# Attention keys in chunks of 128, 128 and 16 instead of 96, 96 and 80, with the small queries of two heads worked on together

## The chip, the cores and the metric

The kernel runs on one core of a Trainium2 chip. The metric is the device time of one execution in microseconds (us). The engines are called as in the profile: PE (matmul; PEld is its weight load), DVE (vector), ACT (scalar activations), POOL (GpSimd) and SP (which only issues DMAs here).

## What is computed

One layer of an encoder over 272 tokens: 16 meta tokens and 256 real ones, 2048 features. All numbers are fp32. Eight heads of group A attend to a window of the token grid and to the meta tokens; eight heads of group B are latent attention over all tokens. Meta tokens are dropped at the end.

```python
hn = rmsnorm(h, mix_norm_g)
q_a, k_a, v_a, cq, ckv, k_pe = split(hn @ w_in)
out_a = neighbourhood_attention(rmsnorm(q_a), rmsnorm(k_a), v_a, na_rpb, na_meta_bias)
out_b = mla_attention(cq, ckv, k_pe, ...)        # softmax(q k^T) v, q and k of 192 dims
mix = concatenate([rmsnorm(out_a), rmsnorm(out_b)])
h = h + mix @ w_out
h = h + conv_glu(rmsnorm(h), w_gate, w_up, conv_w, conv_b, w_down)
return h[:, N_META:]
```

The convolution of the MLP reaches one position to each side, so of the meta tokens only the last one's output is needed. The kernel keeps the real tokens first and the meta tokens behind them in reverse, and computes queries for 258 positions (`NT`): 256 real ones and two more, the *small queries*. Keys and values exist for all 272 (`L`).

## The kernel before

**Numbers.** Every fp32 matrix is split into a rounded fp32r part `hi` and the rest `lo`, and a product is three matmuls (hi hi, hi lo, lo hi; `product3`, `mm3`). Weights come by DMA in pieces of 128 x 1024 into five `raw` buffers; ACT copies each half piece of 512 columns to `whi`, DVE subtracts and writes `wlo`, each with three buffers. PE then streams the 128 x 128 blocks (lines 369 to 371, in the MLP lines 1268 and 1269).

**Order.** The program is recorded by a planner (`Flow`): each piece of work is a generator that asks for an engine with a cost (`ACT`, `TT`, `TS`, `STT`, `COPY`, `RED`, `PTT`, `MM`, `TR` hold the costs), waits for events, and takes buffers from `Slots`. The planner starts whatever can start first by these costs. So the order on each engine is fixed when the program is built, and a change of costs or buffers moves the instructions around it. On the chip each engine takes its queue in this order and waits by semaphores.

**Stages.** First the latent projections, then four pairs of heads, then the output projection (`out_b`, `out_a`) and the MLP. A pair streams the weights of group A's queries, of group B's queries, keys and values (`up`), and of group A's keys and values; its attention work stands between these matmuls on PE. In the order of PE's queue the pairs read as weights with attention blocks among them. `na_head` and `mla_head` spawn three jobs a head: two query tiles of 128 rows (`na_tile`, `mla_tile`) and the small queries of two rows (`na_small`; `mla_tile` with `rows` = 2). Each job makes scores with PE, a softmax with DVE and ACT in `p`, and transposes the probabilities:

```python
CW = 96
LP = 3 * CW
def p_transposed(p, rows, PT, q0, slots):
    yield from TR([(pt[:CW, j * P : j * P + rows], p[:rows, j * CW : (j + 1) * CW]) for j in range(3)])
    ...
    yield from split_plain(PT[:, 0, :, q0 : q0 + rows], PT[:, 1, :, q0 : q0 + rows], src)
```

So the 272 keys are three chunks of 96 rows, the last padded with zeros. `PT` holds the transposed probabilities of one head for all 258 queries, hi and lo, three chunks. `attend` multiplies them with the values: three chunks of three matmuls are nine matmuls of 258 columns, the result is split to `oa` or `ob`, and POOL adds its square to `sum_a` or `sum_b` for the group's RMS norm. `ones_sum` of `sum_b` (a matmul with ones) starts the chain that scales the output projection of group B; the planner lets head h attend after head h - 1 has been added.

The norms of the queries need sums of squares over the 128 or 192 dims. For the tiles ACT sums them along transposed rows; for the small queries PE multiplies `sq2` and `sqm` with a column of ones in fp32, two matmuls a pair in group A (`na_queries`), four in group B (`mla_queries`).

## Time and profile before

| | |
|---|---|
| three runs, median (lowest to highest) | 1144.75 us (1144.36 to 1145.29) |
| the profiled execution's own time | 1144.01 us |
| its span, first to last instruction | 1142.2 us |
| busy: PE, PEld, DVE, ACT, POOL | 1136.7, 1071.1, 812.8, 659.8, 107.7 us |
| matmul records on PE | 8160 |
| chain that ended last | PE 97% |
| clock granted to PE | 1.0 in full |

The latent projections take the first 30 us, the four pairs the time from 30 to about 310 us, 62 us each; then come the output projection and, to the end, the MLP. A matmul's duration in the profile overlaps with the next one's, so what a matmul costs is read from the distance between starts. In a timeline row a group of instructions in sequence has one start, one length and its count.

### The profile page before, as it was taken

What the parts mean: (1) busy time and instruction counts of PE and PEld (TensorE: products, weight loads), DVE (VectorE), ACT (ScalarE), POOL (GpSimd) and SP (SyncE); (2) the same over time, 40 slices, a digit from 0 to 9 for tenths busy, and PEclk for the clock granted to TensorE, in tenths of its full rate; (3) what the DMA queues carried; (4) which work ended last, traced back from release to release, by engine and by line L of the source; (5) the groups of instructions that cost most, each with busy time, mean ns of one, the idle gap of its engine ahead of it and who ended that gap; (6) DMA issues with size and microseconds to landing.
All of it is one profiled execution on the core that took longest, in us unless ns stands there. A gap on an engine that the chain in (4) does not pass through costs nothing.

```text
span 1142.2 us, 21907 instructions
## 1 busy us (share of the span) xinstructions
PE 1136.7 (100%) x8160; PEld 1071.1 (94%) x8160; DVE 812.8 (71%) x1724; ACT 659.8 (58%) x1430; POOL 107.7 (9%) x118
## 2 busy tenths in 40 slices
PE   9999999999999999999999999999999999999998
PEld 8999999999999999999999999999999888888888
DVE  8779696979977866777677767776776755555553
ACT  8677787868645655555555555555555544444442
POOL 0010001010224600010001000100010000000000
PEclk9999999999999999999999999999999999999999
DMA  9543434444555556555555555555555566766662
GB/s 330 184 133 111 158 130 140 139 143 132 188 180 177 181 176 195 189 180 188 186 189 178 192 187 188 177 192 187 187 180 190 174 193 205 211 198 195 198 195 74
DMA packets 63054, 203.62 MB, mean 178 GB/s; under 512 B 6882, under 2 KB 13412, under 8 KB 62948
## 3 DMA queue, kind: packets, MB, share of 16 engines
q1 hardware_dynamic: 62804, 202.11, 55.1%
q8 instruction: 64, 1.05, 0.4%
q14 instruction: 42, 0.34, 0.1%
q10 hardware_dynamic: 144, 0.12, 0.0%
HBM read 200.10 MB, written 2.10 MB: 177 GB/s over the span
## 4 chain that ended last, share of the span: by engine, by line
PE 97%; ACT 1%; issue 1%; DVE 1%; DMA 0%; POOL 0%; DVEq 0%; POOLq 0%
PE bank L1268 27%; PE bank L369 16%; PE bank L370 16%; PE bank L371 16%; PE bank L1269 14%; PE bank L246 5%; PE bank L252 2%; ACT whi L206 1%; ACT hl L206 0%; DMA vecs<-in_vecs 0%; DVE hl L218 0%; DVE wlo L210 0%; ACT scr L206 0%; POOL kr L234 0%; ACT bias L206 0%
## 5 line engine op out<-in xcount | busy, mean ns | idle before, releaser
L210 DVE TENSOR_TENSOR wlo<-raw,whi 128x512 fp32r<-128x512 f32 (+1 forms) x737 | 521.7, 718 | 260.1 <-ACT whi L206 257.2
L206 ACT ACTIVATE whi<-raw 128x512 fp32r<-128x512 f32 (+1 forms) x737 | 458.2, 629 | 396.3 <-PE bank L1268 179.3
L369 PE MATMUL bank<-hl,whi 128*128 128x258 f32 (+1 forms) x1232 | 357.4, 290 | 0.5 <-ACT whi L206 0.3
L370 PE MATMUL bank<-hl,whi 128*128 128x258 f32 (+1 forms) x1232 | 351.4, 285 | 0.1
L371 PE MATMUL bank<-hl,wlo 128*128 128x258 f32 (+1 forms) x1232 | 350.2, 284 | 0.5 <-DVE wlo L210 0.4
L1268 PE MATMUL bank<-hl,whi 128*128 128x512 f32 x704 | 246.3, 392 | 0.0
L371 PEld LDWEIGHTS bank<-hl,wlo 128*128 128x128 f32 x1232 | 235.2, 191 | 1.7 <-DVE wlo L210 1.1
L369 PEld LDWEIGHTS bank<-hl,whi 128*128 128x128 f32 x1232 | 232.7, 189 | 2.7 <-ACT whi L206 1.0
L370 PEld LDWEIGHTS bank<-hl,whi 128*128 128x128 f32 x1232 | 234.3, 190 | 0.5 <-DVE hl L218 0.3
L1268 PE MATMUL bank<-act,whi 128*128 128x512 f32 x660 | 228.8, 391 | 0.0
L1269 PE MATMUL bank<-hl,wlo 128*128 128x256 f32 x704 | 197.8, 281 | 0.0
L1269 PE MATMUL bank<-act,wlo 128*128 128x256 f32 x660 | 185.1, 280 | 0.0
L1268 PEld LDWEIGHTS bank<-hl,whi 128*128 128x128 f32 x704 | 132.1, 188 | 28.7
L1268 PEld LDWEIGHTS bank<-act,whi 128*128 128x128 f32 x660 | 123.5, 187 | 26.8
L1269 PEld LDWEIGHTS bank<-hl,wlo 128*128 128x128 f32 x704 | 132.9, 189 | 0.0
L1269 PEld LDWEIGHTS bank<-act,wlo 128*128 128x128 f32 x660 | 125.0, 189 | 0.0
L234 POOL TENSOR_TENSOR mt<-mt,s 128x256 f32<-128x256 f32 x44 | 41.6, 966 | 459.6 <-ACT mt L206 459.6
L218 DVE SCALAR_TENSOR_TENSOR mt<-mt,vecs,mt 128x256 f32<-128x256 f32 x88 | 40.3, 479 | 0.0
L369 PE MATMUL bank<-ob,whi 128*128 128x258 f32 x128 | 37.1, 290 | 0.0
L370 PE MATMUL bank<-ob,whi 128*128 128x258 f32 x128 | 36.4, 284 | 0.0
L371 PE MATMUL bank<-ob,wlo 128*128 128x258 f32 x128 | 36.0, 281 | 0.0
L206 ACT ACTIVATE scr<-scr 128x272 f32<-128x272 f32 x77 | 32.6, 423 | 5.1 <-DVE scr L218 3.7
(207 smaller groups left out, 1196.3 us busy)
## 6 DMA issues: line engine op xcount, KB each, us to landing
raw<-in_w_gate SPq DMA_DIRECT2D x88, 512.0 KB, 4.3
raw<-in_w_up SPq DMA_DIRECT2D x88, 512.0 KB, 4.4
raw<-in_w_down SPq DMA_DIRECT2D x80, 512.0 KB, 4.4
raw<-in_w_in SPq DMA_DIRECT2D x54, 512.0 KB, 4.2
raw<-in_w_out SPq DMA_DIRECT2D x32, 512.0 KB, 4.3
raw<-in_w_down SPq DMA_DIRECT2D x16, 256.0 KB, 3.3
raw<-in_w_cq SPq DMA_DIRECT2D x7, 512.0 KB, 5.6
bias<-in_na_bias SPq DMA_DIRECT2D x8, 272.0 KB, 4.3
```

The source lines that it names most:

```text
L206: nc.scalar.activation(out, in_, f, **kw)
L210: nc.vector.tensor_tensor(out, a, b, op)
L218: nc.vector.scalar_tensor_tensor(out, a, s, b, op0, op1)
L234: nc.gpsimd.tensor_tensor(out, a, b, op)
L246: nc.tensor.matmul(o, l, r, start=start, stop=stop)
L252: nc.tensor.transpose(o, i, ident[:n, :n])
L369: nc.tensor.matmul(ps, whi, xhi, start=start, stop=False)
L370: nc.tensor.matmul(ps, whi, xlo, start=False, stop=False)
L371: nc.tensor.matmul(ps, wlo, xhi, start=False, stop=stop)
L1268: nc.tensor.matmul(ps, whi, x, start=start, stop=False)
L1269: nc.tensor.matmul(ps[:, :n], wlo, x[:, 0, :], start=False, stop=stop)
```

## The change

The keys are cut into chunks of 128, 128 and the 16 meta tokens. The third chunk is used as one matmul with three copies of the meta tokens in its rows: 32 rows apart stand hi, hi and lo of the values against hi, lo and hi of the probabilities (rows between are zero; `KP` = 80 rows), so one matmul gives all three products. `attend` then has one matmul for the meta tokens and six for the two chunks, seven instead of nine; in group A the six cover only the 256 real queries, since the small queries there attend to meta tokens alone.

The copies are made where the probabilities are normalised (`normalized` writes the 256 columns and then three times the 16) and where group A's values are scaled (`na_values`). `split_chunks` splits the transposed chunks in two steps each on ACT and DVE instead of one.

The small queries of two heads are worked on once a pair, as four rows (head 0's two, head 1's two). Their queries stand in `qs`, where each head's two columns have zeros at the other head's place, so that the scores of both heads accumulate in the same four rows. POOL copies them there (`small_queries`). The sums of squares are two or four fp32r matmuls of two columns, of a split that POOL makes (`small_sums`). `mla_small` and `na_small` run after the second head's keys are there, and both heads' `attend` wait for them (`ev_few`). `PT` holds two heads; there are two instead of three one-head tiles.

```diff
-CW = 96
-LP = 3 * CW
+CW = 32
+KP = 2 * CW + N_META
+LP = L + 3 * CW
...
+    def thrice(row):
+        out = row[:, L : L + 3 * CW].rearrange("p (i x) -> p i x", i=3)[:, :, :N_META]
+        return out, repeated(row[:, SEQ:L], 3)
...
-    pts = Slots(tiles(apool, 3, [CW, 2, 3, NT], "pt", F32R))
+    pts = Slots(tiles(apool, 2, [P, 2, 5, NT], "pt", F32R))
+    qss = tiles(apool, 2, [P, 36], "qs", F32R)
+    sq8 = tiles(apool, 2, [P, 8], "sq8")
+    sq8r = tiles(apool, 2, [P, 2, 8], "sq8r", F32R)
...
+    def chunks_transposed(t, pt):
+        yield from TR(
+            [(pt[:, :P], t[:, :P]), (pt[:, P : 2 * P], t[:, P:SEQ]), last_transposed(t, pt)]
+        )
+    def last_transposed(t, pt):
+        return pt[:KP, 2 * P : 3 * P], t[:, L : L + KP]
+    def split_chunks(out, src, lo):
+        yield from ACT(out[:, 0:2], src[:, 0:2], AF.Copy)
+        yield from TT(out[:, 3:5], src[:, 0:2], out[:, 0:2].bitcast(F32), ALU.subtract)
+        yield from split_last(out[:, 2], src[:, 2], lo)
+    def split_last(out, src, lo):
+        yield from ACT(out[:KP], src[:KP], AF.Copy)
+        e = slice(lo * CW, lo * CW + N_META)
+        yield from TT(out[e], src[e], out[e].bitcast(F32), ALU.subtract)
+    def normalized(p, w, a, n=P):
+        out, src = thrice(p)
+        if a < SEQ:
+            yield from TS(p[:n, a:SEQ], p[:n, a:SEQ], w, None, ALU.mult)
+        yield from TS(out[:n], src[:n], w, None, ALU.mult)
...
-        items = []
-        for j in range(3):
+        items = [(o_, V[:KP, 2], PT[:KP, 2], True, False)]
+        for j in range(2):
             items += product3(
-                o_, (Vh[:, j, :], Vl[:, j, :]), (PT[:, 0, j, :], PT[:, 1, j, :]), j == 0, j == 2
+                o[:, :n], (V[:, j], V[:, 3 + j]), (PT[:, j, :n], PT[:, 3 + j, :n]), False, j == 1
             )
...
+    def small_queries(s):
+        for ev in s.ev_qs:
+            yield ev
+        t = s.qs[:, :24].rearrange("p (l c x) -> p l c x", l=2, c=2)
+        for i in range(2):
+            yield "pool", 150
+            nc.gpsimd.tensor_copy(t[:, i, :, 0:2], s.q[:, :, i, SEQ:NT])
+        fl.set(s.ev_small)
+    def small_sums(q8, n):
+        f, r = q8
+        yield "pool", 150
+        nc.gpsimd.tensor_copy(r[:, 0, : 4 * n], f[:, : 4 * n])
+        yield from PTT(
+            r[:, 1, : 4 * n], f[:, : 4 * n], r[:, 0, : 4 * n].bitcast(F32), ALU.subtract
+        )
...
+            [(ss[:4, 0:2], r[:, i, 4 * g : 4 * g + 4], ones_r[:, 0:2], (g, i) == m[0], (g, i) == m[-1])
+             for g, i in m]
...
-        yield from TS(p[:, :L], p[:, :L], w[:, 2:3], None, ALU.mult)
+        yield from normalized(p, w[:, 2:3], 0)
...
-        yield from p_transposed(p, 2, PT, SEQ, few)
+        pt = yield from one(tps)
+        yield from TR([last_transposed(p, pt)])
+        fl.put(probs, p)
+        yield from split_small(PT, 2, pt)
...
+        if c == 1:
+            fl.spawn(na_small(s, pr, s.PT, s.ev_few))
         for ev in done:
             yield ev
         fl.put(bias, B)
+        yield s.ev_few
...
-            yield from MM([(ss[:2, c : c + 1], sq2[:, c, :], ones[:, 0:1], True, True) for c in range(2)])
+        ss = yield from small_sums(q8, 1)
...
+        for c in range(2):
+            k, kp = s.k[c], s.kp[c]
+            q = [s.qs[:, 12 * i + 4 * c : 12 * i + 4 * c + 4] for i in range(3)]
+            items += product3(S_, q[:2], (k[:, 0, :], k[:, 1, :]), c == 0, False)
+            items += [(S_, q[2], kp[:, 0, :], False, False), (S_, q[2], kp[:, 1, :], False, c == 1)]
```

In the built program PE has 8055 matmul instructions instead of 8119, DVE 1779 instructions instead of 1726, ACT 1397 instead of 1353, and POOL 163 instead of 123; the DMAs are the same but for the shape of `meta_bias`. Line numbers of the changed kernel are 4 to 12 higher at the helpers (`TT` 214 for 210, `MM` 250 for 246, `TR` 256 for 252, `mm3` 381 to 383 for 369 to 371).

More of the change, by code (lines that the diff above doesn't have):

```diff
@@ L868, in na_head @@
         yield ev_B
[L869 to L870 removed]
+        if c == 0:
+            s.PT = yield from one(pts)
+            fl.set(s.ev_PT)
+        yield s.ev_PT
+        done = [Event() for _ in range(2)]
         for i in range(2):
[L872 to L873 removed]
+            fl.spawn(na_tile(s, c, i, B, s.PT, done[i]))
+        if c == 1:
+            fl.spawn(na_small(s, pr, s.PT, s.ev_few))
         for ev in done:
@@ L954, in mla_queries @@
             fl.put(tps, pt)
-        ss = yield from one(sps)
-        for c in range(2):
-            yield from MM(
-                [(ss[:2, c : c + 1], sq2[:, c, :], ones[:, 0:1], True, False),
-                 (ss[:2, c : c + 1], m[:, c, :], ones[:, 0:1], False, True)]
-            )
-        fl.put(sqm, m)
+        ss = yield from small_sums(q8, 2)
         v = yield from one(v6)
```

254 lines of the change are left out of this document (157 added, 97 removed).

## The prediction

> **What bounds the kernel now.** I read the page first, then the waits of PE, then the stretches of one pair of heads, then PE's rows one by one. The page and PE's waits:
>
> ```profile
> PE 1136.7 (100%) x8160; PEld 1071.1 (94%) x8160; DVE 812.8 (71%) x1724; ACT 659.8 (58%) x1430; POOL 107.7 (9%) x118
> PE 97%; ACT 1%; issue 1%; DVE 1%; DMA 0%; POOL 0%; DVEq 0%; POOLq 0%
> PE bank L371 <- DVE wlo L210: 0.4, 2, 0.2
> ```
>
> PE is the bound: it is 97% of the chain that ended last, and it waits for almost nothing. An instruction taken off PE's queue is worth the distance to the next start that it took, if the other engines keep up. Whether they do is read from the stretches of the third pair (columns: stretch and its length, then busy time of PE, PEld, DVE, ACT, POOL):
>
> ```profile
> 188.00:197.40 9.40, 9.40 (x80) 9.12 (x80) 4.67 (x12) 8.15 (x33) 0.76 (x1) 1.00 0.37 119
> 197.40:240.00 42.60, 42.60 (x353) 41.37 (x353) 41.48 (x120) 35.21 (x102) 3.88 (x3) 1.00 0.35 113
> 240.00:252.00 12.00, 12.00 (x102) 11.84 (x101) 7.53 (x15) 7.35 (x18) 1.49 (x2) 1.00 0.60 199
> ```
>
> From 197.4 to 240 DVE has 1.1 us free in 42.6; in the other 21.4 us it has 9.2 free. So in the attention part DVE is nearly as full as PE, and only the split weights that it has ready save PE from waiting. Where that reserve runs out in this pair, and where it is still there:
>
> ```profile
> 204.01 0.69 DVE L210 TENSOR_TENSOR wlo<-raw,whi 128x512 fp32r<-128x512 f32 x1
> 204.55 0.29 PE L370 MATMUL bank<-hl,whi 128*128 128x272 f32 x1
> 204.75 0.40 PE L371 MATMUL bank<-hl,wlo 128*128 128x272 f32 x1
> 236.00 0.68 DVE L210 TENSOR_TENSOR wlo<-raw,whi 128x512 fp32r<-128x512 f32 x1
> 239.31 0.28 PE L371 MATMUL bank<-hl,wlo 128*128 128x258 f32 x1
> ```
>
> The half piece split at 204.01, called C below, is done at 204.70 and used at 204.75: L371 starts 0.20 us behind L370 where 0.125 is usual. The one split at 236.00 lies 2.63 us before its use.
>
> **PE's part of the change.** Its prices are distances between starts:
>
> ```profile
> 223.03 1.24 PE L246 MATMUL bank<-pt,mv 96*128 96x258 f32 x9
> 224.11 0.29 PE L369 MATMUL bank<-hl,whi 128*128 128x272 f32 x1
> ```
>
> Next the two small trios behind each other (`2*96`: transposes of two rows; `128*2 128x16`: small scores of group A), and a trio of transposes from 128 rows:
>
> ```profile
> 228.87 0.29 PE L371 MATMUL bank<-hl,wlo 128*128 128x272 f32 x1
> 229.09 0.30 PE L252 MATMUL bank<-consts,p 2*96 2x2 f32 x3
> 229.32 0.23 PE L246 MATMUL bank<-nak,naq 128*2 128x16 f32 x3
> 229.40 0.37 PE L369 MATMUL bank<-hl,whi 128*128 128x272 f32 x1
> 229.61 0.29 PE L370 MATMUL bank<-hl,whi 128*128 128x272 f32 x1
> ```
>
> ```profile
> 212.38 0.29 PE L371 MATMUL bank<-hl,wlo 128*128 128x272 f32 x1
> 212.51 0.49 PE L252 MATMUL bank<-consts,p 128*96 128x128 f32 x3
> 212.76 0.37 PE L369 MATMUL bank<-hl,whi 128*128 128x272 f32 x1
> 212.97 0.29 PE L370 MATMUL bank<-hl,whi 128*128 128x272 f32 x1
> ```
>
> Attends: nine matmuls take 224.11 - 223.03 = 1.08 us, 0.12 each; seven take 0.84. Four heads a pair (two of each group): 4 x 0.24 = 0.96 us.
>
> Transposes: the two small trios cost 229.61 - 228.87 less two ordinary distances of 0.125, so 0.49, of which 0.08 are the scores' (229.32 to 229.40) and 0.41 the transposes'; three from 128 rows cost 212.97 - 212.38 - 0.25 = 0.34. In a pair, group A's two small trios (0.82) become one transpose. No lone one is in the trace; a third of a trio is 0.11, its bounds are 0.03 and the whole trio's 0.34. I take 0.11, since each further one in a trio only adds its own time: gain 0.71 (0.48 to 0.79). Group B's two trios (0.82) become one trio from 128 rows: gain 0.48. The transposes of the 128-row tiles and of the values keep their number.
>
> The small sums of squares of group B:
>
> ```profile
> 202.44 0.29 PE L371 MATMUL bank<-hl,wlo 128*128 128x272 f32 x1
> 202.66 0.19 PE L246 MATMUL bank<-consts,cols 128*2 128x1 f32 x2
> ...
> 203.16 0.29 PE L370 MATMUL bank<-hl,whi 128*128 128x272 f32 x1
> ```
>
> These four fp32 matmuls cost 203.16 - 202.44 - 0.25 = 0.47; four fp32r ones replace them. The nearest row is the small scores' trio 128x16: 0.08 to the next start, and 0.085 lost at the one after (229.40 to 229.61). Four then cost about 0.2, and 0.1 to 0.47 as bounds: gain 0.27 (0 to 0.37). Group A has two instead of four; its old pair I take at two thirds of B's, 0.31, the new one at 0.13: gain 0.18 (0 to 0.25). The scores of the small queries stay at six and ten matmuls a pair, the value projection at eighteen: nothing.
>
> Sum: 0.96 + 0.71 + 0.48 + 0.27 + 0.18 = 2.60 us a pair, **10.4 us for four pairs** (bounds 4 x 1.92 = 7.7 and 4 x 2.85 = 11.4).
>
> **What DVE gets.** The rows that a tile's work is made of:
>
> ```profile
> L210 DVE TENSOR_TENSOR pt<-bank,pt 96x384 fp32r<-96x384 f32 x32 | 17.1, 543 | 1.1 <-ACT pt L206 1.1
> L214 DVE TENSOR_SCALAR p<-p,cols 128x272 f32<-128x272 f32 x32 | 10.8, 346 | 0.0
> L210 DVE TENSOR_TENSOR act<-mt,act 128x256 fp32r<-128x256 f32 x44 | 18.3, 416 | 0.5 <-ACT act L206 0.5
> L214 DVE TENSOR_SCALAR few<-few,cols 2x16 f32<-2x16 f32 x8 | 1.7, 215 | 0.0
> L210 DVE TENSOR_TENSOR scr<-kr,scr 128x272 f32<-128x272 f32 x8 | 3.4, 428 | 0.0
> L218 DVE SCALAR_TENSOR_TENSOR v<-bank,emc_s 2x2 f32<-2x2 f32 x4 | 0.6, 140 | 0.0
> ```
>
> Each of eight tiles a pair has 543 ns replaced by 416 and a 128-column piece of about 280 (between 416 and the 128 ns fewer columns of the 543 row), and 346 replaced by about 330 and 215: 0.35 us more. With the values' split in two, 8 x 0.35 + 0.7 = 3.5 us; the small work done once a pair instead of twice takes back about 1.0. So 2.5 us more on DVE, where 10.3 us of the 64 shown are free, but mostly outside 197.4 to 240. Twelve more POOL instructions a pair stand beside PE. What matters is what stands ahead of a split whose reserve is out. Before, on DVE in the third pair, the rows up to C, which is the first `wlo_89` (`mqr`: rotary queries, `late`: keys, `emc_s`: the small queries' epsilon):
>
> ```order
> L210 TENSOR_TENSOR mqr_212<-scr_132,mqr_212 64x258
> L218 SCALAR_TENSOR_TENSOR scr_136<-scr_136,gains,scr_131 128x272
> L210 TENSOR_TENSOR late_118<-scr_135,late_118 128x272
> L210 TENSOR_TENSOR mqr_212<-scr_132,mqr_212 64x258
> L210 TENSOR_TENSOR late_117<-scr_136,late_117 128x272
> L218 SCALAR_TENSOR_TENSOR v_179<-cols_167,emc_c 128x4
> L210 TENSOR_TENSOR wlo_89<-raw_80,whi_86 128x512
> L218 SCALAR_TENSOR_TENSOR v_179<-bank_77,emc_s 2x2
> L210 TENSOR_TENSOR scr_131<-kr,scr_131 128x272
> ```
>
> And in the changed kernel at the same place:
>
> ```order
> L214 TENSOR_TENSOR mqr_216<-scr_130,mqr_216 64x258
> L222 SCALAR_TENSOR_TENSOR scr_133<-scr_133,gains,scr_134 128x272
> L214 TENSOR_TENSOR late_118<-scr_131,late_118 128x272
> L214 TENSOR_TENSOR mqr_216<-scr_130,mqr_216 64x258
> L214 TENSOR_TENSOR late_117<-scr_133,late_117 128x272
> L214 TENSOR_TENSOR mv<-bank_72,mv 16x256
> L214 TENSOR_TENSOR scr_134<-kr,scr_134 128x272
> L222 SCALAR_TENSOR_TENSOR v_187<-cols_173,emc_c 128x4
> L222 SCALAR_TENSOR_TENSOR scr_131<-bank_77,sqx 128x272
> L222 SCALAR_TENSOR_TENSOR v_187<-bank_76,emc_s 4x1
> L214 TENSOR_TENSOR wlo_89<-raw_80,whi_86 128x512 x2
> ```
>
> C now stands behind the `kr` product and the `emc_s` step too (the `mv` piece stood further up before, and of the two `sqx` steps one has moved up and one down): 428 + 140 ns later by their durations, while PE comes 0.45 earlier by both groups' sums of squares. The wait for C grows by up to 1.0 us; I take 0.75, since the step that moved up went into DVE's free time. In the second and fourth pair C stands ahead of these, and the half behind it comes later instead; an attend has moved ahead of the place there, so I take 0.3. Together 2 x 0.75 + 2 x 0.3 = **2.1 us back** (0 to 3.6).
>
> **The end of the last pair.** The sums of squares of group B need the last head's attend, which goes over ACT and POOL to the `sum_b` matmul:
>
> ```profile
> 295.01 1.33 PE L246 MATMUL bank<-pt,mv 96*128 96x258 f32 x9
> 297.47 0.39 ACT L206 ACTIVATE scr<-bank 128x258 f32<-128x258 f32 x1
> 297.94 1.33 POOL L234 TENSOR_TENSOR sum_b<-sum_b,scr 128x258 f32<-128x258 f32 x1 [8.68 <-ACT scr L206]
> 299.95 0.60 PE L246 MATMUL bank<-sum_b,consts 128*128 128x258 f32 x2
> ```
>
> From the attend's end (296.34) to POOL's (299.27) 2.9 us pass; before, 21 matmuls of the output projection and three trios stand between, so PE doesn't wait. PE's rows up to `sum_b` before, with the attend 26 rows above the last (`ob`: group B's outputs, streamed through the projection):
>
> ```order
> L246 MATMUL bank_76<-nak_204,naq_202 2x16 x3
> L369 MATMUL bank_73<-ob_192,whi_86 128x258
> L370 MATMUL bank_73<-ob_192,whi_86 128x258
> L371 MATMUL bank_73<-ob_192,wlo_89 128x258
> L252 MATMUL bank_79<-consts,p_140 96x128 x3
> L369 MATMUL bank_75<-ob_192,whi_86 128x258
> L370 MATMUL bank_75<-ob_192,whi_86 128x258
> L371 MATMUL bank_75<-ob_192,wlo_89 128x258
> L369 MATMUL bank_73<-ob_194,whi_87 128x258
> L370 MATMUL bank_73<-ob_194,whi_87 128x258
> L371 MATMUL bank_73<-ob_194,wlo_90 128x258
> L246 MATMUL bank_77<-sum_b,consts 128x258
> ```
>
> Now, with the attend in the first row:
>
> ```order
> L250 MATMUL bank_76<-pt_157,mv 128x258 x7
> L381 MATMUL bank_73<-ob_206,whi_87 128x258
> L382 MATMUL bank_73<-ob_206,whi_87 128x258
> L383 MATMUL bank_73<-ob_206,wlo_90 128x258
> L381 MATMUL bank_75<-ob_206,whi_87 128x258
> L382 MATMUL bank_75<-ob_206,whi_87 128x258
> L383 MATMUL bank_75<-ob_206,wlo_90 128x258
> L256 MATMUL bank_79<-consts,p_139 80x128
> L256 MATMUL bank_78<-consts,p_140 128x128 x2
> L256 MATMUL bank_78<-consts,p_140 80x128
> L250 MATMUL bank_77<-sum_b,consts 128x258
> ```
>
> The attend has moved down to 10 rows above. Six matmuls (0.73) and four transposes (0.45) are left, so PE waits 2.9 - 1.2 = 1.7 us, once; less if the square is taken sooner (0.6 us lay before it). I take **1.5** (0.5 to 2.5).
>
> **Sum.** -10.4 + 2.1 + 1.5 = -6.8 us. Against the profiled execution's own 1144.01 us that is 1137.2; the median of the three runs lies 0.74 higher at 1144.75, which gives 1137.9. About 0.2% (2.3 us) is what a measurement of this kernel can tell from no change.
>
> **Rivals.**
> *No new wait.* DVE's 9 us of room outside the full stretch take the added work, C comes no later than before, and the sums chain is shorter. For it: PE's waits of 0.9 us in all now. Then 10.4 to 11.4 us are gained: 1133.4 to 1134.4. Against it: both places above.
> *POOL in DVE's way.* The new POOL steps fall in the full stretch:
>
> ```profile
> 304.63 1.11 POOL L234 TENSOR_TENSOR sum_a<-sum_a,scr 128x258 f32<-128x258 f32 x1 [5.36 <-ACT scr L206]
> 305.11 1.19 DVE L210 TENSOR_TENSOR wlo<-raw,whi 128x512 fp32r<-128x512 f32 x1
> L900 POOL MEMSET sqm<- 128x4 f32 x1 | 0.2, 223 | 0.0
> ```
>
> A split beside a POOL addition took 1.19 us instead of 0.69. If each of the four steps that come at C (two copies of queries, a cast, a difference) costs DVE the 0.22 us of a small POOL row, PE waits 0.9 us more a pair, 3.6 in all: 1141.5. Against it: the steps have 4 to 8 elements a partition. (The Trainium skill, "SBUF — State Buffer", section "SBUF: two separate sides", says that a DVE instruction with two SBUF inputs and a GpSimd instruction that reads SBUF share a port pair under an exclusive lock; the two rows agree. By that rule the price is that of this rival.)
> *DVE becomes the clock, and the kernel slower.* If the 2.5 us fall into 197.4 to 240, where 1.1 are free, and the reserve (2.63 us at 239.3, none at C) is spent, DVE's stretch sets a pair's time: it gets 2.5 - 1.1 = 1.4 us longer, and PE's gain is lost. 4 x 1.4 + 1.5 = 7.1 us slower: 1151.9. It decides once the splits come over 2.6 us later against PE at the stretch's end. Against it: the changed order moves the last attend of group A into the free part.
> That the change would not do what it says is excluded by the built program: 64 fewer matmul instructions, 32 of attends, 32 transposes.
>
> **Chances.** Forecast (1135 to 1140) 0.56, no new wait 0.20, POOL in the way 0.15, DVE as the clock 0.09. The range 1133.4 to 1142.5 takes in the first three and leaves the slow rival out. Faster by over 0.2% (under 1142.5): 0.56 + 0.20 + 0.12; the rest of the POOL case and a little of the slow one are within 0.2%.
>
> **What would show it.** Right: attends with seven starts in 0.84 us, one small transpose at about 0.11, PE's waits for `wlo` near 0.8 us at C in the first and third pair, a wait of 1 to 2 us at `sum_b`. Wrong: a pair that takes PE as long as before, waits spread over many splits in the attention part, or POOL steps of over 0.3 us.

## The result, and the profile after

The changed kernel takes 1146.88 us (median of 20 runs, 1145.77 to 1148.37) where the kernel before takes 1144.66 us (20 runs on the same chips, 1144.20 to 1145.33): 1.0019 times as long, with a 95% interval of 1.0012 to 1.0026. It was forecast at 1137.9. The profiled execution took 1147.30 us with a span of 1145.3, against 1144.01 and 1142.2 before, so 3.1 us of span are to be explained here. Busy times and the chain of the page:

```profile
PE 1130.8 (99%) x8072; PEld 1064.0 (93%) x8072; DVE 826.2 (72%) x1777; ACT 659.1 (58%) x1466; POOL 118.3 (10%) x158
PE 87%; DVE 6%; ACT 5%; issue 1%; DMA 1%; POOL 0%; SPq 0%; POOLq 0%; ACTq 0%
```

PE is busy for 5.9 us less than before, in a span that is longer: it waits now, and the chain has gone from 97% PE to 87%. The waits of PE (us in total, times, longest; left out are 1.2 us for `em`, which the kernel before has too, and two of 0.2 and 0.3 us):

```profile
PE bank L383 <- DVE wlo L214: 3.6, 7, 0.9
PE bank L256 <- DVE pt L214: 2.3, 3, 1.0
PE bank L381 <- ACT whi L210: 1.6, 1, 1.6
PE bank L256 <- DVE nav L214: 1.1, 1, 1.1
PE bank L250 <- POOL sum_b L238: 0.8, 1, 0.8
```

Before, `wlo` had 0.4 us of this and transposes (L252 there) none. `wlo` is the wait at C, as forecast. The waits of transposes for `pt` and `nav` weren't forecast at all: PE wants one of the two transposition banks that DVE hasn't finished splitting. The one wait for `whi` stands in the projection's first pieces at 11 us; another execution of the same order (the POOL run below) doesn't have it, so it belongs to this execution.

The stretches of the third pair, with the middle one of the same length as before:

```profile
188.90:198.30 9.40, 9.40 (x79) 9.09 (x78) 5.42 (x15) 8.55 (x34) 2.49 (x8) 1.00 0.52 180
198.30:240.90 42.60, 41.71 (x341) 40.59 (x340) 41.15 (x121) 33.52 (x101) 2.61 (x5) 1.00 0.35 112
240.90:250.60 9.70, 9.69 (x81) 9.39 (x80) 8.40 (x24) 6.78 (x22) 2.71 (x2) 1.00 0.71 227
```

DVE (third engine) is as full as it was, 41.15 of 42.60, and busier on both sides; PE (first) now has 0.9 us in which it waits.

**PE's own part.** An attend with seven matmuls, and C in the third pair on PE and on DVE:

```profile
229.93 1.00 PE L250 MATMUL bank<-pt,mv 80*128 80x258 f32 x7
230.77 0.28 PE L381 MATMUL bank<-hl,whi 128*128 128x272 f32 x1
```

```profile
204.10 0.41 DVE L214 TENSOR_TENSOR mv<-bank,mv 16x256 fp32r<-16x256 f32 x1
204.53 0.44 DVE L214 TENSOR_TENSOR scr<-kr,scr 128x272 f32<-128x272 f32 x1
...
204.96 0.44 DVE L222 SCALAR_TENSOR_TENSOR scr<-bank,sqx 128x272 f32<-128x272 f32 x1
205.32 0.14 DVE L222 SCALAR_TENSOR_TENSOR v<-bank,emc_s 4x1 f32<-4x1 f32 x1
205.38 1.27 DVE L214 TENSOR_TENSOR wlo<-raw,whi 128x512 fp32r<-128x512 f32 x2
```

```profile
204.93 0.29 PE L382 MATMUL bank<-hl,whi 128*128 128x272 f32 x1
206.10 0.39 PE L383 MATMUL bank<-hl,wlo 128*128 128x272 f32 x1 [0.89 <-DVE wlo L214]
```

The attend takes 230.77 - 229.93 = 0.84 us, as forecast. C is late by 206.10 - 204.93 - 0.125 = 1.05 us behind the steps named in the forecast. Working the same out for every start in the trace (all distances that are at least 0.3 us above the usual one, which is about 0.125 us behind 258 or 272 columns, 0.23 behind 512 and 0.11 behind a transpose), PE loses 12.7 us in the changed kernel and 2.0 before:

| where PE waits | more than before, us | forecast |
|---|---|---|
| C in the four pairs: 1.05, 0.63, 1.05, 0.59 | 3.3 | 2.1 |
| end of the last pair: 1.24, 0.68, 1.21, 0.99, 0.41 | 4.5 | 1.5 |
| second pair, at 176 and 182 us: 0.68 and 0.90 | 1.6 | - |
| first pieces, this execution | 1.2 | - |
| all | 10.6 | 3.6 |
| what is left of the span (1132.6 against 1140.2) | -7.6 | -10.4 |
| span | +3.1 | -6.8 |

The last line but one still holds the shorter waits.

**The end of the last pair**, PE's rows that wait:

```profile
299.98 0.55 PE L256 MATMUL bank<-consts,p 128*128 128x128 f32 x3 [1.07 <-DVE nav L214]
302.60 0.31 PE L256 MATMUL bank<-consts,p 128*80 128x128 f32 x1 [0.52 <-DVE pt L214]
303.92 0.55 PE L256 MATMUL bank<-consts,p 128*128 128x128 f32 x3 [1.01 <-DVE pt L214]
305.30 0.70 PE L250 MATMUL bank<-sum_b,consts 128*128 128x258 f32 x2 [0.83 <-POOL sum_b L238]
```

The last of them is the one that was forecast. The first waits for the bank with the second head's transposed values, whose split is on ACT and DVE (a row joins steps in sequence under the first one's shape: 298.02 is the last step of the first head's values and the second step of the second's):

```profile
295.69 0.64 ACT L210 ACTIVATE nav<-bank 128x256 fp32r<-128x256 f32 x2
298.80 0.27 ACT L210 ACTIVATE nav<-bank 80x128 fp32r<-80x128 f32 x1 [0.55 <-DVE nav L214]
```

```profile
298.02 0.74 DVE L214 TENSOR_TENSOR nav<-bank,nav 16x128 fp32r<-16x128 f32 x2
...
298.75 0.85 DVE L214 TENSOR_TENSOR wlo<-raw,whi 128x512 fp32r<-128x512 f32 x1
299.63 0.29 DVE L214 TENSOR_TENSOR nav<-bank,nav 16x128 fp32r<-16x128 f32 x1
```

Four steps go to and fro, and each stands behind what else its engine has: ACT waits for DVE, DVE does a `wlo` in between. From the last of three transposes to the end of the last step of their split a bank is held 3.27 us (mean of the forty blocks of 128 rows, out of the trace's rows), where it was 1.32 before. What DVE and ACT now do for a tile, and for group B's values:

```profile
L214 DVE TENSOR_TENSOR pt<-bank,pt 128x256 fp32r<-128x256 f32 x32 | 13.1, 419 | 0.9 <-ACT pt L210 0.5
L218 DVE TENSOR_SCALAR p<-p,cols 128x256 f32<-128x256 f32 x32 | 11.6, 376 | 0.0
L214 DVE TENSOR_TENSOR pt<-bank,pt 16x128 fp32r<-16x128 f32 x32 | 8.9, 283 | 1.8 <-ACT pt L210 1.0
L210 ACT ACTIVATE pt<-bank 80x128 fp32r<-80x128 f32 x32 | 8.6, 270 | 9.1 <-DVE pt L214 8.9
L218 DVE TENSOR_SCALAR p<-p,cols 128x48 f32<-128x48 f32 x32 | 8.0, 261 | 0.1
L210 ACT ACTIVATE mv<-bank 16x256 fp32r<-16x256 f32 x8 | 3.0, 370 | 0.1
```

A tile costs DVE 419 + 283 + 376 + 261 - 543 - 346 = 450 ns more, where 350 was forecast, and DVE's busy time has grown by 13.4 us, 3.35 a pair instead of 2.5. (A sum of durations counts too much here: successive instructions overlap in the rows, 204.96 + 0.44 against a next start at 205.32. So where runs are compared below, DVE's busy time is given.)

### The profile page after: what moved, and what is told of

It reads as the page before. It is cut to its first block, busy times and chain, and to the rows that moved or that the text cites. A ratio compares the mean times of both kernels' runs of the same rounds, so it can differ in the third digit from the quotient of the medians.

```text
span 1145.3 us, 21863 instructions
## 1 busy us (share of the span) xinstructions
PE 1130.8 (99%) x8072; PEld 1064.0 (93%) x8072; DVE 826.2 (72%) x1777; ACT 659.1 (58%) x1466; POOL 118.3 (10%) x158
## 3 DMA queue, kind: packets, MB, share of 16 engines
q8 instruction: 63, 1.03, 0.4%
## 4 chain that ended last, share of the span: by engine, by line
PE 87%; DVE 6%; ACT 5%; issue 1%; DMA 1%; POOL 0%; SPq 0%; POOLq 0%; ACTq 0%
PE bank L1407 27%; PE bank L1408 14%; PE bank L383 14%; PE bank L382 14%; PE bank L381 14%; PE bank L250 2%; DVE wlo L214 2%; ACT scr L210 1%; DVE scr L222 1%; ACT whi L210 1%; PE bank L256 1%; ACT bank L210 1%; DVE pt L214 1%; DVE p L218 1%; DMA scr<-in_xT 1%
## 5 line engine op out<-in xcount | busy, mean ns | idle before, releaser
L210 ACT ACTIVATE pt<-bank 128x256 fp32r<-128x256 f32 (+3 forms) x88 | 23.7, 281 | 27.1 <-DVE pt L214 20.0
```

Of the source, the lines that this page charges most:

```text
L210: nc.scalar.activation(out, in_, f, **kw)
```

## The experiments

Four theories stood against each other. **D**: DVE's added work of 3.35 us a pair is what PE waits for. **S**: it is the split in four steps to and fro, and the long hold of the two transposition banks. **J**: it is the joint small queries, for which both heads' attends wait. **O**: it is the order that the planner gives, whatever the work. Besides, the **POOL** rival of the prediction. Each result is the median of the runs, and the ratio to the kernel before on the same chip with its 95% interval.

### Which half of the change

*Chunks alone* (`e2_chunks`):

```diff
-    pts = Slots(tiles(apool, 2, [P, 2, 5, NT], "pt", F32R))
+    pts = Slots(tiles(apool, 3, [P, 5, NT], "pt", F32R))
...
-        if c == 1:
-            fl.spawn(na_small(s, pr, s.PT, s.ev_few))
+        fl.spawn(na_small(s, c, h, PT, done[2]))
```

> The chunks alone: keys in chunks of 128, 128 and three copies of 16, but each head's small queries by themselves, two rows, as before (PT for one head, three buffers; fp32 sums of squares; no POOL copies). PE gains 0.96 us a pair at the attends and some 0.5 at group A's small transposes, 5.8 us in all. Theories S and D: the waits stay, since the four-step splits and DVE's work stay (even more small work on DVE), so 1144 to 1148, no faster than before. Theory J: the waits at the end of the last pair and at C go, and the time is 1139 to 1140.

1151.15 us, 1.0058 (1.0045 to 1.0070). *Joint small queries alone* (`e3_small`):

```diff
-CW = 32
+CW = 96
...
-        yield from split_small(PT, 0, pt)
+        yield from small_transposed(p, PT, probs)   # chunks of 96, split in one step
```

> The joint small queries alone: chunks of 96, 96 and 80 and one-step splits as before, but the small queries of two heads in four rows, with POOL's copies, fp32r sums and the common wait of both attends. PE gains some 0.41 + 0.41 (two small trios fewer a pair) + 0.45 (sums) = 1.27 us a pair, 5 us in all; DVE has about 1 us a pair less. Theories S and D: no new waits, 1139 to 1141. Theory J: the end of the last pair keeps its waits of 3 to 4.5 us and C comes late, 1143 to 1146. The POOL rival: as J, by the waits for wlo.

1143.41 us, 0.9986 (0.9977 to 0.9995). The chunks lose 6.5 us and the joint small queries win 1.2. So J isn't what makes the changed kernel slower. But its time for the small queries alone (1143 to 1146) is what came, and not the 1139 to 1141 of S and D: 0.76, 0.33 and 0.71 us of waiting at the end of the last pair come with them, and C is late by 0.34 us in the third pair. With the long distances taken out as above, 1137.1 us are left of their span of 1141.7, 3.1 less than before where 5 were expected. The halves don't add up (+5.3 against +2.2 together). The chunks alone are slower than any theory had said: 1139.1 us are left of their span of 1149.6, only 1.1 less than before where 5.8 were expected, and the rest is waits, at other places than the changed kernel's. Both halves keep three `PT` tiles of one head; so the two tiles of two heads, which only the changed kernel has, aren't needed for a loss.

### POOL

*New small POOL steps twice* (`e4_pool_twice`; the copies and casts, seven of the nine new steps a pair, 28 instructions in all):

```diff
-            nc.gpsimd.tensor_copy(t[:, i, :, 0:2], s.q[:, :, i, SEQ:NT])
+            for _ in range(2):
+                nc.gpsimd.tensor_copy(t[:, i, :, 0:2], s.q[:, :, i, SEQ:NT])
```

> The changed kernel with each of its new small POOL steps on the small queries (copies and casts, 9 of 12 a pair, without the differences) issued twice; the order on all other engines is the same. That is some 2.5 us more a pair on POOL. The POOL rival (small POOL steps hold up DVE's two-input operations, or who waits for them is on the path): 2 to 4 us slower than the changed kernel, 1149 to 1151. Theories S, D and J: within 0.7 us of the changed kernel's 1146.9.

1146.51 us, 1.0020 (1.0011 to 1.0029), the changed kernel's time. POOL's busy time in it, beside the 118.3 of the page above, and the two longest sorts of the small steps in the changed kernel:

```profile
PE 1133.1 (99%) x8072; PEld 1066.6 (93%) x8072; DVE 826.0 (72%) x1777; ACT 659.9 (58%) x1466; POOL 125.7 (11%) x186
```

```profile
L784 POOL CAST qs<-naq 128x4 fp32r<-128x4 f32 x8 | 3.3, 424 | 17.4 <-ACT naq L210 17.2
L791 POOL CAST sq8r<-sq 128x8 fp32r<-128x8 f32 x4 | 1.9, 471 | 0.0
```

7.4 us more on POOL leave DVE's busy time and the result where they were. The POOL rival falls.

### The split in four steps

*Both hi parts first* (`e1_hi_first`):

```diff
         yield from ACT(out[:, 0:2], src[:, 0:2], AF.Copy)
+        yield from ACT(out[:KP, 2], src[:KP, 2], AF.Copy)
         yield from TT(out[:, 3:5], src[:, 0:2], out[:, 0:2].bitcast(F32), ALU.subtract)
-        yield from split_last(out[:, 2], src[:, 2], lo)
+        e = slice(lo * CW, lo * CW + N_META)
+        yield from TT(out[e, 2], src[e, 2], out[e, 2].bitcast(F32), ALU.subtract)
```

> The changed kernel, but a split of transposed chunks copies both hi parts on ACT first and then subtracts both lo parts on DVE (ACT, ACT, DVE, DVE instead of ACT, DVE, ACT, DVE). The work is the same, the hand-overs between the engines are fewer. Theory S (the split in four alternating steps is what PE waits for: ACT stood 20 us waiting for DVE's pt, and the transposition banks are held longer): ACT's wait for pt falls under 5 us, most of PE's waits in front of transposes go, and the time falls by 3 to 6 us, to 1141 to 1144. Theory D (DVE's 3.4 us more a pair is what PE waits for): DVE's work is unchanged, so the time stays within 1 us of 1146.9. Theory J (the joint small queries hold back both heads' attends): the waits at the end of the last pair stay at 4 to 5 us, time 1145 to 1147.

1149.39 us, 1.0040 (1.0028 to 1.0053). *One hi step over all three chunks* (`e16_one_hi_step`), the same with `ACT(out[:, 0:3], src, AF.Copy)` as its only ACT step (the third transpose then covers 128 columns):

> The changed kernel (three copies, seven matmuls, same DVE work), but one ACT step copies the hi part of all three transposed chunks, followed by the two DVE subtractions: three steps with one hand-over instead of four with three. Theory S: the banks are held under 2.5 us instead of 3.27, 3 to 5 us faster than the changed kernel, 1142 to 1144. Theory D: within 1 us of 1146.9. Theory O: 1143 to 1151.

1146.91 us, 1.0022 (1.0013 to 1.0030). *Four steps in the kernel before* (`e10_before_four_steps`):

```diff
-        yield from split_plain(PT[:, 0, :, q0 : q0 + rows], PT[:, 1, :, q0 : q0 + rows], src)
+        for j in (slice(0, 2), slice(2, 3)) if rows == P else (slice(0, 3),):
+            q = slice(q0, q0 + rows)
+            yield from split_plain(PT[:, 0, j, q], PT[:, 1, j, q], src[:, j])
```

> The kernel before, its chunks of 96 kept, but each split of the tiles' transposed probabilities made as in the changed kernel: ACT and DVE on two chunks, then ACT and DVE on the third. DVE gets some 8 x 0.13 = 1.0 us more a pair (a second step's fixed cost), and the planner orders anew. Theory S: the banks are held 2.5 to 3 us instead of 1.3, and the time rises by 4 to 7 us, to 1149 to 1152. Theory D: 1.0 us more on DVE, a third of what cost 5.9 us when the row maximum was taken twice, so 1 to 2 us more, 1145.5 to 1147.

1146.11 us, 1.0013 (1.0004 to 1.0022). The waits of ACT, first of the changed kernel, then of the one with one hi step:

```profile
ACT pt L210 <- DVE pt L214: 20.0, 26, 2.0
```

```profile
ACT pt L210 <- DVE pt L214: 5.8, 6, 1.9
```

Most of ACT's standstill goes and the hold falls from 3.27 to 2.53 us, and the time doesn't move. With both hi parts first ACT's wait falls as far (6.0 us) but the hold hardly (3.15 us), and the kernel is 2.5 us slower. Four steps in the kernel before raise its hold from 1.32 to 2.44 us and cost 1.6 us. That is far from S's 4 to 7 and inside D's 1 to 2 (DVE is busy for 3.2 us more); but the planner orders anew in these three runs, and order alone moves the time as much (below). So a price of several us for the four steps shows nowhere, and S isn't the main cause as far as these runs go; a smaller share of it isn't excluded. (ACT gets no data from DVE here. The Trainium skill, "PSUM — Partial Sum Buffer", section "PSUM bank collisions raise a hardware error", says that the compiler's scheduler adds a dependency between any two instructions of different engines that touch the same bank and quadrant, reads against reads too. The trace fits that: both steps read the bank, and the 20.0 us are there. Both also write into one `pt` tile, and no run here tells the two reasons apart.)

### DVE's load at an unchanged order

In these five the planner counts what isn't issued, or doesn't count what is issued twice, so the order on every engine stays that of the kernel they start from. *Keys' norm without its two refining steps, in the changed kernel and in the one before* (`e5_after_less_dve`, `e6_before_less_dve`):

```diff
-        yield from STT(a, v, -0.5, a, ALU.mult, ALU.mult)
-        yield from STT(out, a, 1.5, out, ALU.add, ALU.mult)
+            for _ in range(2):          # for the keys only
+                yield "dve", 68 + 1.04 * size(out)
```

> The changed kernel without the two refining DVE steps of the keys' norm (the reciprocal square root of the four keys' sums of squares a pair is left at ACT's value); the planner still counts them, so the order of everything else, on every engine, is that of the changed kernel. DVE gets 8 x 0.44 = 3.5 us less a pair, about what the change added (3.35). Theory D (DVE's load is what PE waits for): the waits at C (1.05, 0.63, 1.05, 0.59 us) and those inside the pairs go, those at the end of the last pair shrink, 5 to 8 us faster than the changed kernel, 1139 to 1142. Theory O (the order that the planner gives is what costs, and it is unchanged here): 1145 to 1147. Theory S (four steps in turn): the banks' splits still alternate, 1144 to 1147.

> The same taken from the kernel before: the two refining DVE steps of the keys' norm aren't issued, the order is that of before. It is what the run on the changed kernel is to be set against. Theory D: PE hardly waits before (0.9 us in all), so at most 1 us is gained, 1143.5 to 1144.7; the changed kernel with the same relief is then the faster of the two by 2 to 5 us. Theory O: also 1143.5 to 1144.7, and the changed kernel with the relief stays slower.

1143.99 us, 0.9996 (0.9987 to 1.0004), and 1144.03 us, 0.9992 (0.9984 to 1.0001): 2.9 us from the changed kernel, and 0.5 from the one before, which its interval doesn't tell from nothing. *Row maximum left out in the changed kernel* (`e18_after_no_max`):

```diff
-        yield from RED(w[:, 0:1], S_, ALU.max, negate=True)
+        yield "dve", 68 + 1.04 * L
```

> The changed kernel without the row maximum of its eight tiles a pair (the softmax is then taken against whatever number stands there): 3.4 us less a pair on DVE in the attention tiles, which is what the change added there; the planner still counts it, so the order is unchanged. Taking as much from the keys' norm gave 2.9 us, and left the waits at C and the end of the last pair. Theory D, with the place deciding: taken from the tiles it gives 5 to 7 us, 1140 to 1142, and the waits of the last pair shrink. Theory O (the order of the last pair and at C costs by itself): 1143.5 to 1145, the waits of the last pair stay at 4 us.

1144.55 us, 0.9997 (0.9988 to 1.0006): 2.3 us gained. *Row maximum twice in the kernel before* (`e7_before_more_dve`) and *in the fastest version* (`e17_full_rows_more_dve`, told with its start further down):

```diff
         yield from RED(w[:, 0:1], sb[:, :L], ALU.max, negate=True)
+        nc.vector.tensor_reduce(w[:, 0:1], sb[:, :L], AX.X, ALU.max, negate=True)
```

> The kernel before with DVE's row maximum of each of the eight tiles a pair taken twice (the same result; 8 x 0.42 = 3.4 us more a pair on DVE, in the attention tiles, where the change adds its own), the order of everything else unchanged. Theory D: PE's queue is as long as before and DVE's full stretch has 1.1 us free of 3.4, so waits of 1.5 to 2.5 us a pair come up at C and at the splits behind it, 1150 to 1155. Theories O and S: no change of order and no split in four steps, so 1144.5 to 1146.

> The fastest kernel so far (two steps, two copies, full rows: 1139.9) with DVE's row maximum of each of the eight tiles a pair taken twice, 3.4 us more a pair on DVE in the attention tiles, as the change adds it; the order of everything else is unchanged. Theory D: the 1139.9 go back to where the changed kernel is, 5 to 9 us slower, 1145 to 1149. If DVE's load isn't the cause: within 1.5 us of 1139.9.

1150.49 us, 1.0052 (1.0039 to 1.0064), 5.9 us lost; and 1144.52 us, 0.9999 (0.9991 to 1.0008), 4.6 lost against 1139.94, a little less than the 5 to 9 expected. DVE's busy time moved by less than the 3.4 us a pair of the durations: it is 11.3 and 11.7 us up in these two runs (2.8 and 2.9 a pair), and 10.6 and 8.9 us down with the lighter keys' norm and without the row maximum in the changed kernel (2.7 and 2.2 a pair), where the change had added 13.4. The third pair's middle stretch of the kernel before with the doubled maximum, and where its PE then waits most:

```profile
201.00:244.00 43.00, 42.20 (x344) 40.24 (x343) 42.58 (x122) 34.35 (x100) 3.90 (x3) 1.00 0.32 102
```

```profile
PE bank L252 <- DVE pt L210: 2.0, 4, 0.5
```

DVE is busy for 42.58 of 43.00 us, and PE no longer for all of it. So 2.8 to 2.9 us a pair more on DVE, with the order unchanged, cost 1.2 to 1.5 us a pair: D holds as a cause. (The second maximum also makes each tile's chain 0.43 us longer; the runs don't part that from the load.) Taken away from the changed kernel, 2.2 to 2.7 us a pair give back only 0.6 to 0.7 a pair. The end of the last pair without the row maximum shows why:

```profile
297.01 0.55 PE L256 MATMUL bank<-consts,p 128*128 128x128 f32 x3 [0.66 <-DVE nav L214]
299.68 0.31 PE L256 MATMUL bank<-consts,p 128*80 128x128 f32 x1 [0.57 <-DVE pt L214]
301.01 0.55 PE L256 MATMUL bank<-consts,p 128*128 128x128 f32 x3 [1.02 <-DVE pt L214]
302.38 1.23 PE L250 MATMUL bank<-sum_b,consts 128*128 128x258 f32 x2 [0.82 <-POOL sum_b L238]
```

The first has fallen from 1.07 to 0.66 us; the other three are the changed kernel's within 0.05 us, with 8.9 us less on DVE in all. That is what O expected of this run. So most of the waiting there, and at C, comes from what stands in which order. C, on DVE of the changed kernel with the lighter keys' norm:

```profile
198.93 0.69 DVE L214 TENSOR_TENSOR mv<-bank,mv 128x512 fp32r<-128x512 f32 x1 [1.01 <-ACT mv L210]
...
201.84 0.44 DVE L214 TENSOR_TENSOR late<-scr,late 128x272 fp32r<-128x272 f32 x1 [0.43 <-ACT late L210]
...
203.57 1.27 DVE L214 TENSOR_TENSOR wlo<-raw,whi 128x512 fp32r<-128x512 f32 x2
```

DVE has time here (1.01 and 0.43 us idle), but it waits for ACT, whose queue holds one copy of the meta tokens' values more than before (two of 370 ns, the row above), and the split of C stands behind it all. PE waits 1.03 us there, as in the changed kernel.

### The order

*One constant of the planner*, in the kernel before (`e11_before_order`), the changed one (`e12_after_order`) and the fastest version (`e15_full_rows_order`):

```diff
-    TO_PE, FROM_PE, OTHER = 700.0, 200.0, 140.0
+    TO_PE, FROM_PE, OTHER = 700.0, 220.0, 140.0
```

> The kernel before with one constant of the planner changed (what it adds for a hand-over from PE: 220 instead of 200 ns), so that the same work comes in another order on PE, DVE and ACT. Theory O (order alone moves the time by as much as the change did): 2 us or more from 1144.6 in either direction. Theories S and D: within 1 us, 1143.6 to 1145.6.

> The same on the changed kernel: the hand-over from PE planned at 220 instead of 200 ns. Theory O: the changed kernel has more to lose by an unlucky order, so 2 to 4 us from 1146.9 in either direction, and with luck below 1144. Theories S and D: the waits move but their sum stays, 1145.5 to 1148.5.

> The two-step kernel with full rows, with the planner's hand-over from PE at 220 instead of 200 ns (the constant that cost the kernel before 1.9 us and the changed kernel 4.3). Theory O: 2 to 4 us from the 200 ns version in either direction. Theory D: DVE has room here, as in the kernel before, so at most 2 us slower.

1146.43 us, 1.0018 (1.0009 to 1.0027), so 1.9 us lost; 1151.17 us, 1.0056 (1.0042 to 1.0070), 4.3 lost; 1140.81 us, 0.9969 (0.9957 to 0.9980), 0.9 lost against 1139.94. The same work in another order moves the time by about as much as the change did in two of the three (O expected 2 to 4 us of the fastest version too, and 0.9 came), and it moved the changed kernel most, in one try each. So order alone can cost this much, and O holds that far. That an unlucky order is what made the changed kernel slow isn't shown: all three moves are losses, and none of the changed kernel's other orders in these runs is faster than its first.

### Less work for DVE, and a version that beats both

*The three copies written by ACT* (`e8_copies_on_act`):

```diff
-        yield from TS(out[:n], src[:n], w, None, ALU.mult)
+        yield from ACT(out[:n], src[:n], AF.Copy, scale=w)
```

> The changed kernel with the three normalised copies of the meta tokens' probabilities (128 x 48, 261 ns on DVE, eight a pair, and the small queries' 4 x 48) written by ACT, which scales them by the same column, instead of DVE. DVE gets 2.1 us + 0.4 us less a pair, ACT about as much more; the planner orders anew. Theory D: three quarters of the change's added DVE work is gone, and 3 to 6 us come back, 1141 to 1144. Theory O: another order, 1145 to 1149. Theory S: ACT's queue gets longer, no gain, 1146 to 1149.

1145.92 us, 1.0009 (1.0000 to 1.0018): 1.0 us gained, less than the 3 to 6 that D gave, in another order and with DVE busy for only 4.6 us less; C is still late by 1.05 us in all four pairs. *Two copies, one ACT and one DVE step for a tile's split* (`e9_two_steps`; it also goes back to three `PT` tiles of one head, and group B's values need one ACT copy of the meta tokens instead of two):

```diff
+    def copied(p, n=P):                  # behind the exponential
+        out, src = twice(p[:n])
+        yield from ACT(out, src, AF.Copy)
...
-        yield from split_chunks(PT[:, :, q0 : q0 + P], src, 1)
+        yield from split_plain(PT[:, 0:3, q0 : q0 + P], PT[:, 3:6, q0 : q0 + P], src)
...
-        items = [(o_, V[:KP, 2], PT[:KP, 2], True, False)]
+        items = [(o_, V[:KP, 2], PT[:KP, 2], True, False)]           # KP = 48
+        items += [(o_, V[:N_META, 2], PT[:N_META, 5], False, False)]
```

> Chunks of 128, 128 and the meta tokens, joint small queries, but two copies of the meta tokens instead of three (32 rows apart), copied by a small ACT step behind the exponential, so that one DVE step normalises the whole row, and one ACT and one DVE step split all three transposed chunks, as before the change. The meta tokens take two matmuls (hi and lo of the values against hi; hi against lo), so attend has eight matmuls. DVE's load is that of before within 1 us a pair, a transposition bank should be held some 1.4 us again (1.32 before, 3.27 in the changed kernel, mean of the forty 128-row blocks). Theory S (the split in four steps and the long hold of the two banks) and theory D (DVE's load) both give the joint small queries' 1143.4 less 16 x 0.12 us for the eighth matmul: 1140 to 1142, faster than both kernels. Theory O (only the order that the planner happens to give matters): anywhere from 1142 to 1149.

1147.52 us, 1.0024 (1.0015 to 1.0034), with 4.9 us of waits in PE's list where the changed kernel has 11.1: PE itself had become slower. An attend's eight matmuls there, and in the next version, *the two meta-token matmuls over all 128 rows* (`e13_full_rows`):

```diff
-        items = [(o_, V[:KP, 2], PT[:KP, 2], True, False)]
-        items += [(o_, V[:N_META, 2], PT[:N_META, 5], False, False)]
+        items = [(o_, V[:, 2], PT[:, 2], True, False), (o_, V[:, 2], PT[:, 5], False, False)]
```

```profile
188.05 1.60 PE L251 MATMUL bank<-pt,nav 48*128 48x258 f32 x8
189.49 0.29 PE L380 MATMUL bank<-late,whi 128*128 128x258 f32 x1
```

```profile
184.90 1.11 PE L251 MATMUL bank<-pt,nav 128*128 128x258 f32 x8
185.84 0.29 PE L380 MATMUL bank<-late,whi 128*128 128x258 f32 x1
```

> The two-step kernel of the last runs with its two meta-token matmuls over all 128 rows instead of 48 and 16 (the other rows are zeros; values hi and lo against hi, then against lo). There a matmul of 48 or 16 rows took 0.31 us to the next start, one of 128 rows takes 0.12, one of 80 rows 0.15; an attend took 1.53 us, and eight matmuls of full rows should take 0.96. That is 16 x 0.57 = 9.1 us less on PE, with DVE's work and the split in two steps unchanged. Theories S and D (the change's added DVE work and its split in four steps are what ate PE's gain): 1137.5 to 1140, faster than both kernels. Theory O: the new order may eat 2 to 4 us of that, 1140 to 1144.

1139.94 us, 0.9959 (0.9947 to 0.9972): 4.7 us faster than the kernel before and 6.9 faster than the changed one, with an attend of 0.94 instead of 1.44 us to the next start (the expectation's 1.53 has in it 0.09 us by which the attend itself starts later). The order of instructions on PE, DVE and ACT is the same in these two runs, so their 7.6 us are the row counts' alone. Its busy times and its waits for DVE (without `em`):

```profile
PE 1129.3 (99%) x8088; PEld 1066.1 (94%) x8088; DVE 812.7 (71%) x1693; ACT 660.5 (58%) x1462; POOL 118.3 (10%) x158
```

```profile
PE bank L382 <- DVE wlo L215: 2.5, 4, 1.7
PE bank L251 <- DVE late L215: 0.6, 1, 0.6
```

DVE has the 812.8 us of the kernel before again, and no transpose waits. Taking the long distances out as above, 1131.5 us are left of its span of 1137.9, 8.7 less than before: the forecast sum of PE's gains for eight matmuls is 10.4 - 16 x 0.12 = 8.5. *The same with the split in four steps* (`e14_full_rows_four_steps`):

```diff
-        yield from split_plain(PT[:, 0:3, q0 : q0 + P], PT[:, 3:6, q0 : q0 + P], src)
+        for a, b in ((0, 2), (2, 3)):
+            q = slice(q0, q0 + P)
+            yield from split_plain(PT[:, a:b, q], PT[:, 3 + a : 3 + b, q], src[:, a:b])
```

> The same with the split of the tiles' transposed probabilities in four steps (ACT and DVE on two chunks, then ACT and DVE on the third) as in the changed kernel. DVE gets some 8 x 0.13 = 1.0 us more a pair. PE's work is the same. Theory S: the banks are held 2.5 to 3 us, and it is 4 to 7 us slower than with two steps. Theory D: 1 to 2 us slower. Theory O: 2 to 4 us in either direction.

1141.03 us, 0.9968 (0.9956 to 0.9979): 1.1 us slower, at a hold of 2.44 instead of 1.55 us. S's 4 to 7 us don't come here either. DVE is busy for only 0.5 us more (813.2), so its load doesn't explain the 1.1 us; the order changed too.

**What stays open.** The changed kernel is 6.9 us behind the fastest version, 8.8 with the eighth matmul's 1.9. Of these 2.3 to 2.9 came back when 8.9 to 10.6 of the 13.4 us that the change put on DVE were taken away at a given order. The other 6 or so are a remainder, which no run shows by itself. We put it down to the order and the pieces that stand in it: the planner lays out the work by its counts, and with more and smaller pieces its order leaves PE waiting at C and at the end of the last pair. How it divides between the extra ACT copy at C, the longer chains of a tile, the two `PT` tiles of two heads (the fastest version has three of one again, and that wasn't tried alone) and chance wasn't settled; the changed kernel's work came out at 1146.9 to 1151.2 in four orders (the two with the split's steps moved among them), the fastest version's at 1139.9 to 1141.0 in three (one with the split in four steps).

## Why the prediction was wrong

- **PE's gains, 10.4 us: right in their mechanism, and about right in size.** The attend took the forecast 0.84 us. In the fastest version PE had 8.7 us of the 8.5 that are due there. In the changed kernel 7.6 are to be seen, just under the lower bound (7.7); short waits lie among them. In the two halves alone less of the gain is to be seen (3.1 of 5 and 1.1 of 5.8 us), and why isn't settled.
- **C, 2.1 us: right place, too small.** It measured 1.05 and 1.05 us in the first and third pair (0.75 forecast) and 0.63 and 0.59 in the others (0.3): 3.3 in all, within the bound of 3.6. In those two pairs the prediction's own "up to 1.0 us" came nearly whole; the quarter that it took off for a step moved into DVE's free time wasn't there. The forecast looked at what stands ahead of C on DVE and not on ACT, where a second copy of the meta tokens' values had come in; that this copy is the reason is read from the queues, and no run took it out alone.
- **The end of the last pair, 1.5 us: the step that failed most.** The wait at `sum_b` was there, 0.83 us, or 0.99 by the distance. Ahead of it PE waited three times for a transposition bank, 3.1 us together by the distances, which the forecast doesn't have; with 0.4 at an attend behind it, 4.5 us came. It counted the matmuls that would cover POOL's chain and no other chain. Another 1.6 us came in the second pair, for a split at 176 us and a transposition bank at 182, where the forecast has nothing. In the other orders of the changed kernel the end of the last pair costs 2.6 us (both hi parts first) to 5.5 (the planner's constant); in the versions with eight matmuls over full rows it costs from nothing (the fastest) to 2.9 (four steps).
- **DVE, "2.5 us more, mostly outside 197.4 to 240": wrong in the conclusion.** It was 3.35 us a pair, and the 64 us of a pair, of which 10.3 were free, aren't one store: 2.8 us a pair added alone cost the kernel before 5.9 us, though its DVE was idle for more than that in each pair.
- **The rivals.** *No new wait* (0.20) was excluded by the waits. (The 0.9 us of PE's waits that spoke for it left out the 1.2 for `em`.) *POOL in DVE's way* (0.15) fell with the doubled steps, though single POOL steps did take more than 0.3 us (471 and 424 ns for two sorts); there are nine new steps a pair, not twelve. *DVE becomes the clock* (0.09) was the nearest: the doubled maximum is its mechanism by itself, and a pair took 63.5 us there instead of 62.0. It had the deciding point wrong: the splits at a stretch's end weren't what PE waited for, since `wlo` kept its 0.4 us in that run, and the transposition banks were. And its 1151.9 took PE's gain to be lost whole, while 7.6 us of it are to be seen and the waits beside them are only in part DVE's sum. Too much of the chance lay on the forecast: it read the new order at two places, and nothing in its rows told how far that order, whose effect the runs put at 0.9 to 4.3 us, would leave PE waiting elsewhere.
- **The signs.** "A pair that takes PE as long as before" is nearly what came: C's waits in pairs one and three, which end at 82.82 and 206.10 us, lie 2 x 61.6 us apart, where a pair took 62.0. Of the signs of being right, the attend and C's wait (0.89 us in the row above) came; the wait at `sum_b`, 0.83 us, stayed under its 1 to 2. The lone small transpose took 0.11 us in the first pair (0.03 to the next start, 0.08 lost behind it), and 0.26 and 0.19 in the next two with the delay in front of it.

## What to carry to other kernels

A saving on the bounding engine is only worth what the second engine lets through: add work to that one alone, at an unchanged order, and see what it costs before you trade for it. When a planner sets the order, move one of its constants by a tenth on both kernels first: the scatter of that is the noise in which a change of the same size must be read. And look at what the cheaper form asks of every engine: the version that won here gave up one of the matmuls saved, and kept DVE's and ACT's work as it was.

## What the runs showed of the hardware that was not expected

- In these attends a matmul over 48 or 16 rows took 0.31 us to the next start (`e9_two_steps`), one over 80 rows 0.15 (the changed kernel), one over 128 rows 0.12, each with 258 columns. Zeros in the other rows were worth 7.6 us of time at an unchanged order (1147.52 to 1139.94; 16 attends by 0.50 us are 8.0). The Trainium skill, "TensorEngine Tiling (Array Packing)", section "Key Properties", says that a change of the tiling mode drains TensorE. The rows fit that if few rows mean another mode; nothing here shows the mode itself.
- 20 ns in one constant of the planner, which is no hardware at all, moved the device time by 1.9, 4.3 and 0.9 us.
